# Keys and queries left unnormalised, the gate's silu moved, attention sums batched, last scaling out of place

## The chip, the cores and the metric

The kernel runs on one core of a Trainium2 chip. Its five engines work side by side, each through its own queue in order: TensorE (PE in the rows, its weight loads PEld), VectorE (DVE), ScalarE (ACT), GpSimd (POOL) and SyncE (SP, which here only issues transfers). The metric is the device time of one execution in microseconds (us).

## What is computed

One layer of a hybrid encoder for two sequences of 512 and 256 tokens, 1024 features, which share the weights. All is in float32. Cut to what matters:

```python
def _deltanet(qkv, z, ...):
    qkv = silu(centred_conv(qkv, conv_w))
    q, k = l2norm(q), l2norm(k)        # t * rsqrt(sum(t*t) + EPS), per token and head
    o = delta_direction(q, k, v, forward) + delta_direction(q, k, v, backward)
    o = o * rsqrt(mean(o * o, -1) + EPS) * norm_w
    return o * silu(z)

def _layer(x, mem, ...):
    proj = rms_norm(x, g_pre_mix) @ w_in
    att = window_attention(aq, ak, av, sink)   # window 128, softmax with one sink per head
    mix = concatenate([att, deltanet(...)], -1) @ w_out
    x = x + rms_norm(mix, g_post_mix)
    x = x + rms_norm(cross_attention(rms_norm(x, g_pre_xa), mem, ...), g_post_xa)
    h = rms_norm(x, g_pre_mlp)
    return x + rms_norm(square(relu(h @ w1)) @ w2, g_post_mlp)
```

## The kernel before, in words

The 768 tokens are six tiles of 128 (tiles 0 to 3 the first sequence, 4 and 5 the second). A large product is made of three matmuls on high and low halves of both operands (lines 187 to 189, 502 and 503, 1089 to 1091, 1165 to 1167); `split` (lines 182, 183) and the weight loader (lines 106 to 108) make these halves: ScalarE copies the high half, VectorE or GpSimd subtracts.

The body is written as generators that are merged or chained; a planner in the compiler then orders each engine's queue by program order and by when it reckons an operand to be ready. So work that stands later in the program fills gaps. The order of the stages:

1. Input norm, projections of attention's queries, keys and values, gates (0 to 97 us of the profile).
2. `proj_dn(0)`, the DeltaNet projections of heads 0 and 1, merged with `window`, the attention (97 to 230). `proj_dn` goes through keys, queries, values; for each head it projects all tokens, convolves along tokens with four VectorE multiply-adds (line 554), applies silu through tanh (557, 558), turns tiles back to token-major on TensorE (563), sums squares (571), takes the root on GpSimd (`rsqrt`, 151 and 152), normalises on VectorE (580), and turns the normalised tiles feature-major again (583, 584).
3. `deltanet(0)` chained with `proj_dn(1)` (230 to 352). `prep` makes for each pair of tiles and both directions a masked exponential E of gate sums (693, 695), multiplies the keys' Gram matrix by it (696) and the key-query product in PSUM by it (697). `inverse` inverts triangular blocks by 30 dependent VectorE steps (719, 723) and small matmuls. `step` is the scan over tiles; `dn_out` normalises its output (867 to 869) and stores it.
4. `deltanet(1)` chained with `fill` (352 to about 505): `proj_z` (the gate, with tanh, line 515 and the scaling 516), the memory's norm and keys and values. TensorE takes these while the inverse and the scan go on.
5. `tail`: output projection (`out_tile`, skewed over tiles, where line 1049 multiplies by the gate), cross-attention, and pre-norms (to 720).
6. The MLP, its second product by a Strassen scheme with seven products (720 to 1180), and `down_last` with `finish`: the last block's product is added to the accumulators (1249), squares are summed on ScalarE (1005), the sum and the root are taken on GpSimd (1007, 151, 152), the gain is multiplied in place (1260), the scaled result is added to the residual (1261) and stored.

PSUM has eight banks; in stages 2 to 4 they are tagged mm (2), tr (1), dnp (2), dns (1) and wn (2). In `window` a head's scores, their transposes and the value product share one bank, taken in turn from wn, wn and dns (line 910 the scores, 914 mask and maximum, 918 exponential, 921 transposes, 924 copy, 926 value product, 930 scaling). A ring of five tiles tagged quad holds MLP weights and at the end the gain and the residuals.

## Time and profile before

| | us |
|---|---|
| median of 3 runs (1231.92 to 1237.18) | 1232.74 |
| the profiled execution, its own time | 1231.01 |
| its span, first to last instruction | 1229.2 |
| TensorE busy | 1128.0 (92%) |
| VectorE busy | 736.4 (60%) |
| ScalarE busy | 529.3 (43%) |
| GpSimd busy | 434.7 (35%) |

The mean granted clock of TensorE is 0.967 of 2.4 GHz. Busy shares are means over stages that have different limits. In the rows, "idle before" in brackets is the time that the engine stood still before an instruction and what ended that; a wait for several things is put down to the last one. Matmuls are pipelined, so the durations of neighbours overlap. Line numbers are those of the kernel before.

### The profile page before, as it was taken

Reading aid. Unit: us, or ns where it says so; the run is one execution under the profiler, and the core shown is the slowest. Engines: PE = TensorE matmul, PEld = TensorE weight load, DVE = VectorE, ACT = ScalarE, POOL = GpSimd, SP = SyncE. Lnnn points to the kernel's source line nnn. Section 1 sums busy time; section 2 is a strip of 40 time slices with the busy share of each in tenths; the row PEclk is TensorE's granted clock in tenths of the full one; section 3 lists DMA queues with packets and bytes.
Section 4 is the critical chain, followed back from the end, with each engine's and each line's share of the span. In section 5 each row is a group of like instructions: output and inputs, shape, how many; then the busy total and the mean of one; then the engine's idle time right before and its main releaser. Section 6 shows DMA issues by size and latency. Waiting matters only on the chain.

```text
span 1229.2 us, 18098 instructions
## 1 busy us (share of the span) xinstructions
PE 1128.0 (92%) x6848; PEld 962.8 (78%) x6848; DVE 736.4 (60%) x1361; ACT 529.3 (43%) x1151; POOL 434.7 (35%) x468
## 2 busy tenths in 40 slices
PE   6998999987988799889898989999999999999994
PEld 5887788866877597578687778888888888888883
DVE  5315776799789723446534736365658565658655
ACT  5346777644565324434434534433323333233321
POOL 5353321234246423011000136343435343535461
PEclk9999999998998789899899999999999999999997
DMA  6355211311113205932722233121213122213212
GB/s 196 97 179 171 86 44 35 96 45 41 36 61 108 74 27 173 289 129 95 222 69 69 87 122 100 39 82 55 84 57 89 44 76 63 86 52 89 82 53 103
DMA packets 106931, 113.85 MB, mean 93 GB/s; under 512 B 8431, under 2 KB 80219, under 8 KB 106843
## 3 DMA queue, kind: packets, MB, share of 16 engines
q1 hardware_dynamic: 99195, 99.55, 26.8%
q10 hardware_dynamic: 7648, 13.13, 2.8%
q8 instruction: 54, 0.88, 0.3%
q14 instruction: 34, 0.28, 0.1%
HBM read 91.27 MB, written 21.39 MB: 92 GB/s over the span
## 4 chain that ended last, share of the span: by engine, by line
PE 42%; issue 4%; POOL 2%; DVE 2%; DMA 1%; ACT 1%; POOLq 0%; DVEq 0%; ACTq 0%
PE up L1165 7%; PE up L1167 7%; PE up L1166 7%; PE y L187 5%; PE y L189 5%; PE y L188 5%; POOL y L1227 1%; DMA raw<-in_xa_wo 1%; PE xa L1126 1%; PE xa L1107 1%; PE mm L1090 1%; PE mm L1091 1%; POOL rs L152 1%; PE mm L1089 1%; ACT junk L1005 0%
## 5 line engine op out<-in xcount | busy, mean ns | idle before, releaser
L108 POOL TENSOR_TENSOR wlo<-raw,whi 128x512 fp32r<-128x512 f32 (+1 forms) x61 | 88.6, 1456 | 149.2 <-ACT whi L107 100.6
L1170 POOL TENSOR_TENSOR hid<-hid 128x256 f32<-128x256 f32 (+1 forms) x64 | 60.8, 951 | 224.3 <-ACT hid L1169 224.1
L189 PE MATMUL y<-w,hl 128*128 128x512 f32 x318 | 123.9, 389 | 0.5 <-DVE hl L183 0.5
L187 PE MATMUL y<-w,hh 128*128 128x512 f32 x318 | 123.7, 389 | 0.0
L188 PE MATMUL y<-w,hh 128*128 128x512 f32 x318 | 123.7, 389 | 0.0
L1209 DVE TENSOR_TENSOR y<-y,y 128x512 f32<-128x512 f32 x72 | 48.9, 683 | 107.4 <-PE y L189 107.4
L108 DVE TENSOR_TENSOR w<-raw,w 128x1024 fp32r<-128x1024 f32 (+1 forms) x58 | 78.4, 1356 | 51.2 <-ACT w L107 51.0
L1169 ACT ACTIVATE hid<-up 128x256 f32<-128x256 f32 (+1 forms) x64 | 31.2, 488 | 179.4 <-PE up L1167 179.4
L1165 PE MATMUL up<-hx0h,w 128*128 128x512 f32 x256 | 101.2, 395 | 1.0 <-DVE hx0l L183 1.0
L1167 PE MATMUL up<-hx0h,w 128*128 128x512 f32 x256 | 100.4, 392 | 0.0
L1166 PE MATMUL up<-hx0l,w 128*128 128x512 f32 x256 | 100.1, 391 | 0.0
L971 POOL TENSOR_TENSOR quad<-quad 128x1024 f32<-128x1024 f32 x28 | 77.9, 2780 | 32.9 <-DVE w L108 14.9
L108 DVE TENSOR_TENSOR w<-quad,w 128x1024 fp32r<-128x1024 f32 x49 | 72.5, 1492 | 12.4 <-ACT w L107 12.4
L1165 PE MATMUL up<-hx4h,w 128*128 128x256 f32 x256 | 72.6, 284 | 4.5 <-ACT hid L1169 4.5
L107 ACT ACTIVATE w<-raw 128x1024 fp32r<-128x1024 f32 (+1 forms) x58 | 55.5, 964 | 43.6 <-DMA raw<-in_w_out 17.2
L1166 PE MATMUL up<-hx4l,w 128*128 128x256 f32 x256 | 72.0, 281 | 0.1
L1167 PE MATMUL up<-hx4h,w 128*128 128x256 f32 x256 | 71.8, 280 | 0.0
L189 PEld LDWEIGHTS y<-w,hl 128*128 128x128 f32 x318 | 59.7, 188 | 13.3 <-DVE hl L183 0.9
L188 PEld LDWEIGHTS y<-w,hh 128*128 128x128 f32 x318 | 59.7, 188 | 12.4
L187 PEld LDWEIGHTS y<-w,hh 128*128 128x128 f32 x318 | 59.7, 188 | 12.4
L182 ACT ACTIVATE hh<-hid 128x768 fp32r<-128x768 f32 x37 | 31.4, 848 | 81.3 <-PE y L188 64.0
L107 ACT ACTIVATE whi<-raw 128x512 fp32r<-128x512 f32 (+1 forms) x61 | 37.8, 623 | 53.1 <-DMA raw<-in_xa_wkv 10.4
(369 smaller groups left out, 3211.2 us busy)
## 6 DMA issues: line engine op xcount, KB each, us to landing
raw<-in_mlp_w SPq DMA_DIRECT2D x36, 512.0 KB, 4.4
quad<-in_mlp_w SPq DMA_DIRECT2D x28, 512.0 KB, 4.7
raw<-in_w_in SPq DMA_DIRECT2D x44, 256.0 KB, 2.9
d_x<-x ACTq DMA_DIRECT2D x12, 512.0 KB, 2.6
x<-d_x SPq DMA_DIRECT2D x12, 512.0 KB, 3.8
x<-in_x_prompt SPq DMA_DIRECT2D x8, 512.0 KB, 3.6
raw<-in_xa_wkv SPq DMA_DIRECT2D x16, 256.0 KB, 2.8
d_att<-parts SPq DMA_DIRECT2D x12, 256.0 KB, 2.0
```

The costliest lines, as they stand in the source:

```text
L107: self.nc.scalar.activation(hi[:, c], raw, AF.Copy)
L108: self.sub(out=lo[:, c], in0=raw, in1=hi[:, c].bitcast(F32), op=ALU.subtract)
L182: nc.scalar.activation(hi, src, AF.Copy)
L187: nc.tensor.matmul(ps, lh, rh, start=first, stop=False)
L188: nc.tensor.matmul(ps, lh, rl, start=False, stop=False)
L189: nc.tensor.matmul(ps, ll, rh, start=False, stop=last)
L971: nc.gpsimd.tensor_tensor(out=out, in0=x, in1=y, op=ALU.subtract)
L1165: nc.tensor.matmul(ps, wh[:, k], hh[:, k], start=k == 0, stop=False)
L1166: nc.tensor.matmul(ps, wh[:, k], hl[:, k], start=False, stop=False)
L1167: nc.tensor.matmul(ps, wl[:, k], hh[:, k], start=False, stop=k == 7)
L1170: nc.gpsimd.tensor_tensor(out=r, in0=r, in1=r, op=ALU.mult)
L1209: nc.vector.tensor_tensor(out=y, in0=y, in1=ps, op=ALU.add)
```

## The change

- `proj_dn` no longer normalises keys and queries. The product of tanh writes feature-major tiles straight into the kept buffers; the second transposes and the product of line 580 are gone. Norms of keys go as factors into the two Gram products (`na`, `a`, by scaled ScalarE copies), into the values (`rv`) and into the gate factor `kdc`; those of the queries go into the output's root in `dn_out` (`sq`).
- The product of line 697 moves from VectorE on PSUM to GpSimd on an SBUF copy.
- `proj_z` stores the raw gate; `out_tile` applies silu.
- `window`: scores are negated and masked with a minimum, so that the negation falls away; the value tiles get a column of ones, so that the value product also gives the sums; four heads share one bank (dns) for value products, and sums, sinks and scaling are done for four heads at once; scores use the two wn banks only. The load of keys and values is two loads.
- `finish` multiplies by the gain into a new tile `yg`; the gain lies in two tiles of another ring; in `rstd` the addition of two sums is a `tensor_scalar` with a pointer operand.

```diff
@@ proj_z
-        th = pool.tile([P, 770], F32, tag="tanh", bufs=1, name="th")
...
         for c, ps in zip((slice(0, 512), slice(512, 768)), out):
-            nc.scalar.activation(th[:, c], ps, AF.Tanh, scale=0.5)
-            nc.vector.scalar_tensor_tensor(out=z[:, c], in0=th[:, c], scalar=1.0, in1=ps, op0=ALU.add, op1=ALU.mult)
-        nc.gpsimd.tensor_scalar(z, z, self.nw, 0.0, ALU.mult, ALU.add)
+            nc.scalar.activation(z[:, c], ps, AF.Copy)
         nc.scalar.dma_start(self.d_z[h], z)
@@ proj_dn
-                nc.vector.scalar_tensor_tensor(out=y, in0=th, scalar=1.0, in1=y, op0=ALU.add, op1=ALU.mult)
+                dst = keep[("QhT", "KhT")[kind]][:, h] if kind < 2 else y
+                spans = [(slice(0, 512), slice(0, 512)), (slice(512, TOK), slice(514, 770))] if kind < 2 else [(slice(0, 770),) * 2]
+                for to, c in spans:
+                    nc.vector.scalar_tensor_tensor(out=dst[:, to], in0=th[:, c], scalar=1.0, in1=y[:, c], op0=ALU.add, op1=ALU.mult)
...
                     if kind == 2:
-                        nc.scalar.activation(keep["V"][:, s0:s0 + nt, h, :], ps3, AF.Copy)
+                        for t in range(nt):
+                            nc.scalar.activation(keep["V"][:, s0 + t, h, :], ps[:, t * P:(t + 1) * P], AF.Copy,
+                                                 scale=keep["rv"][:, s0 + t, h:h + 1])
                         continue
...
-                    nc.vector.tensor_tensor(out=dst, in0=ps3, in1=r.unsqueeze(2).to_broadcast([P, nt, P]), op=ALU.mult)
-                    ps = self.ps("tr")
-                    for t in range(nt):
-                        nc.tensor.transpose(ps[:, t * P:(t + 1) * P], dst[:, t], self.ident)
-                    nc.scalar.activation(dstT[:, h, s0 * P:(s0 + nt) * P], ps[:, :nt * P], AF.Copy)
+                        nc.scalar.activation(keep["Kh"][:, s0:s0 + nt, h, :], ps[:, :nt * P].rearrange("p (t f) -> p t f", f=P), AF.Copy)
+            G = nc.gpsimd
+            if kind == 1:
+                sk, a, rv = keep["sk"], keep["a"], keep["rv"]
+                G.tensor_scalar(sk, sk, EPS, 0.0, ALU.add, ALU.add)
+                G.tensor_tensor(out=a, in0=sk, in1=self.mhalf.unsqueeze(2).to_broadcast([P, NT, 2]), op=ALU.pow)
+                G.tensor_tensor(out=rv, in0=sk, in1=a, op=ALU.mult)
+                G.tensor_tensor(out=a, in0=a, in1=a, op=ALU.mult)
+                G.tensor_scalar(keep["na"], a, -1.0, 0.0, ALU.mult, ALU.add)
+                for d in range(2):
+                    kdc = self.kdc[:, :, 4 * d + 2 * half:4 * d + 2 * half + 2]
+                    G.tensor_tensor(out=kdc, in0=kdc, in1=a, op=ALU.mult)
+            elif kind == 0:
+                G.tensor_scalar(keep["sq"], keep["sq"], EPS, EPS * P * P, ALU.add, ALU.mult)
@@ prep
-        nc.scalar.activation(Gn, ps4(psG), AF.Copy, scale=-1.0)
+        for tt, t in enumerate(ts):
+            for h in range(2):
+                nc.scalar.activation(Gn[:, 2 * tt + h], ps4(psG)[:, 2 * tt + h], AF.Copy, scale=keep["na"][:, t, h:h + 1])
...
+        Pa = pool.tile([P, 4, P], F32, tag="S4", bufs=1, name="Pa")
+        for tt, t in enumerate(ts):
+            for h in range(2):
+                nc.scalar.activation(Pa[:, 2 * tt + h], ps4(psP)[:, 2 * tt + h], AF.Copy, scale=keep["a"][:, t, h:h + 1])
...
-            nc.vector.tensor_tensor(out=E[:, ds], in0=ps4(psP), in1=E[:, ds], op=ALU.mult)
+            nc.gpsimd.tensor_tensor(out=E[:, ds], in0=Pa, in1=E[:, ds], op=ALU.mult)
@@ dn_out
-        r = self.rsqrt(pool, ss, 2, 1.0 / P, EPS, "rso")
-        nc.vector.tensor_tensor(out=O, in0=O, in1=r.unsqueeze(2).to_broadcast([P, 2, P]), op=ALU.mult)
+        nc.gpsimd.tensor_tensor(out=ss, in0=ss, in1=sq[:, t], op=ALU.add)
+        nc.gpsimd.tensor_tensor(out=ss, in0=ss, in1=self.mhalf[:, 0:1].to_broadcast([P, 2]), op=ALU.pow)
+        nc.vector.tensor_tensor(out=O, in0=O, in1=ss.unsqueeze(2).to_broadcast([P, 2, P]), op=ALU.mult)
@@ window (the new loop over heads; load is cut)
+                for jj in range(2):
+                    hs = slice(4 * jj, 4 * jj + 4)
+                    nm = pool.tile([P, 4], F32, tag="nm", bufs=4, name="nm")
+                    es = pool.tile([P, 4], F32, tag="es", bufs=4, name="es")
+                    pv = self.ps("dns", "pv")[:, :260].rearrange("p (h f) -> p h f", h=4)
+                    for x in range(4):
+                        h = 4 * jj + x
+                        ps = self.ps("wn", "wS")
...
+                        nc.vector.tensor_tensor_reduce(out=sc[:, :nk * P], in0=ps[:, :nk * P], in1=mk, scale=-0.125,
+                                                       scalar=self.nsink[:, h:h + 1], op0=ALU.add, op1=ALU.min,
+                                                       accum_out=nm[:, x:x + 1])
+                        nc.scalar.activation(sc[:, :nk * P], sc[:, :nk * P], AF.Exp, bias=nm[:, x:x + 1], scale=-1.0)
...
+                        for b in range(nk):
+                            nc.tensor.matmul(pv[:, x], pT[:, b], vs[:, k0 + b, jj], start=b == 0, stop=b == nk - 1)
+                        yield
+                    nc.gpsimd.tensor_tensor(out=es, in0=nm, in1=self.sink[:, hs], op=ALU.add)
+                    nc.scalar.activation(es, es, AF.Exp)
+                    nc.vector.tensor_tensor(out=es, in0=pv[:, :, 64], in1=es, op=ALU.add)
+                    nc.vector.reciprocal(es, es)
+                    nc.vector.tensor_tensor(out=o[:, hs], in0=pv[:, :, 0:64], in1=es.unsqueeze(2).to_broadcast([P, 4, 64]), op=ALU.mult)
@@ rstd
-            nc.gpsimd.tensor_tensor(out=ss[:, 0:1], in0=ss[:, 0:1], in1=ss[:, 1:2], op=ALU.add)
+            nc.gpsimd.tensor_scalar(ss[:, 0:1], ss[:, 0:1], ss[:, 1:2], 0.0, ALU.add, ALU.add)
@@ out_tile
+        th = pool.tile([P, 4, P], F32, tag="b2", bufs=3, name="zth")
+        nc.scalar.activation(th, zt, AF.Tanh, scale=0.5)
+        nc.vector.scalar_tensor_tensor(out=zt, in0=th, scalar=1.0, in1=zt, op0=ALU.add, op1=ALU.mult)
...
-        nc.vector.tensor_tensor(out=zt, in0=zt, in1=pz.rearrange("p (k c) -> p k c", k=4), op=ALU.mult)
+        nc.vector.scalar_tensor_tensor(out=zt, in0=pz.rearrange("p (k c) -> p k c", k=4), scalar=self.nw, in1=zt,
+                                       op0=ALU.mult, op1=ALU.mult)
@@ down_last
-        gain = self.w2pool.tile([P, D], F32, tag="quad", bufs=5, name="gain")
-        nc.sync.dma_start(gain, self.a["norm_post_mlp"][0].partition_broadcast(P))
+        gain = [pool.tile([P, 512], F32, tag="S", bufs=2, name="gain", padded_shape=[P, 768]) for _ in range(2)]
+        for j in range(2):
+            nc.sync.dma_start(gain[j], self.a["norm_post_mlp"][0][512 * j:512 * j + 512].partition_broadcast(P))
@@ finish
+        yg = self.w2pool.tile([P, D], F32, tag="quad", bufs=5, name="yg")
         r = self.rstd(pool, [ya, yb])
         for j, y in enumerate((ya, yb)):
             c = slice(512 * j, 512 * j + 512)
-            nc.vector.tensor_tensor(out=y, in0=y, in1=gain[:, c], op=ALU.mult)
-            nc.vector.scalar_tensor_tensor(out=x[:, c], in0=y, scalar=r, in1=x[:, c], op0=ALU.mult, op1=ALU.add)
+            nc.vector.tensor_tensor(out=yg[:, c], in0=y, in1=gain[j], op=ALU.mult)
+        for j in range(2):
+            c = slice(512 * j, 512 * j + 512)
+            nc.vector.scalar_tensor_tensor(out=x[:, c], in0=yg[:, c], scalar=r, in1=x[:, c], op0=ALU.mult, op1=ALU.add)
             nc.sync.dma_start(self.row(t)[1][:, c], x[:, c])
```

## Rows read from the trace of the kernel before

**Rows 1.** Head of the page: span; engines' busy us, share, instructions.

```profile
span 1229.2 us, 18098 instructions
...
PE 1128.0 (92%) x6848; PEld 962.8 (78%) x6848; DVE 736.4 (60%) x1361; ACT 529.3 (43%) x1151; POOL 434.7 (35%) x468
```

**Rows 2.** Busy us by stretch: stretch, length, PE, PEld, DVE, ACT, POOL, clock, DMA.

```profile
97.00:230.00 133.00, 126.40 (x879) 110.14 (x878) 89.40 (x326) 99.05 (x310) 32.40 (x37) 1.00 0.26 78
230.00:302.00 72.00, 60.83 (x420) 51.79 (x420) 68.32 (x172) 36.96 (x81) 25.47 (x23) 0.93 0.24 60
...
352.00:420.00 68.00, 52.33 (x347) 43.89 (x345) 65.89 (x158) 36.63 (x82) 40.95 (x36) 0.85 0.26 86
...
480.00:583.00 103.00, 91.70 (x425) 73.15 (x424) 46.05 (x66) 38.30 (x73) 10.20 (x25) 0.97 0.57 186
...
1175.00:1230.00 55.00, 35.81 (x154) 28.31 (x153) 31.91 (x42) 11.27 (x27) 22.55 (x27) 0.87 0.22 77
```

**Rows 3.** Waits of TensorE, 230 to 302 and 352 to 420: us, times, longest.

```profile
PE tr L583 <- DVE room L580: 7.8, 3, 5.6
...
PE wn L187 <- DVE z L515: 5.6, 1, 5.6
PE mm L502 <- DVE z L515: 3.6, 1, 3.6
PE tp L381 <- DVE z L515: 2.7, 1, 2.7
```

**Rows 4.** Timelines of VectorE and TensorE, 470 to 510: start, length, instruction [idle before].

```profile
476.01 0.43 DVE L869 TENSOR_TENSOR O<-O,rs 128x256 f32<-128x256 f32 x1 [0.87 <-POOL rs L152]
...
497.73 0.40 PE L187 MATMUL wn<-hm,whi 128*128 128x512 f32 x1
...
505.46 0.79 PE L187 MATMUL mm<-w,hx4h 128*128 128x512 f32 x1 [0.57 <-ACT hx4h L182]
```

**Rows 5.** Timeline of VectorE in the final scaling, tile 3 of 6, and the end.

```profile
1199.40 0.68 DVE L1249 TENSOR_TENSOR yc<-yc,y 128x512 f32<-128x512 f32 x1
1200.93 0.69 DVE L1260 TENSOR_TENSOR yc<-yc,gain 128x512 f32<-128x512 f32 x1 [0.85 <-ACT junk L1005]
1201.54 0.68 DVE L1249 TENSOR_TENSOR y<-y,y 128x512 f32<-128x512 f32 x1
...
1204.75 0.75 DVE L1261 SCALAR_TENSOR_TENSOR x<-yc,rs,x 128x512 f32<-128x512 f32 x1 [0.99 <-POOL rs L152]
...
1224.85 1.41 DVE L1261 SCALAR_TENSOR_TENSOR x<-y,rs,x 128x512 f32<-128x512 f32 x2 [1.00 <-POOL rs L152]
```

**Rows 6.** Timeline of GpSimd for the same tile.

```profile
1203.11 0.70 POOL L1007 TENSOR_TENSOR ss<-ss 128x1 f32<-128x1 f32 x1 [5.08 <-ACT junk L1005]
1203.89 0.19 POOL L151 TENSOR_SCALAR rs<-ss 128x1 f32<-128x1 f32 x1
1204.17 0.55 POOL L152 TENSOR_TENSOR rs<-rs,mhalf 128x1 f32<-128x1 f32 x1
```

**Rows 7.** Line 515's own view: ns min/median/max, first and last start.

```profile
L515 DVE SCALAR_TENSOR_TENSOR z<-th,mm x4: 406/542/678, 370.5 to 386.8; 128x512 f32<-128x512 f32 x2, 128x256 f32<-128x256 f32 x2
```

**Rows 8.** VectorE's groups, 230 to 480: count, busy us, mean ns, idle.

```profile
L697 DVE TENSOR_TENSOR E<-dnp,E 128x512 f32<-128x512 f32 x12 | 7.9, 678 | 0.0
```

**Rows 9.** Timeline of TensorE: first transposes of two and of four tiles.

```profile
227.39 0.44 PE L563 MATMUL tr<-ident,y 128*128 128x128 f32 x2 [0.16 <-DVE y L558]
...
228.30 0.66 PE L563 MATMUL tr<-ident,y 128*128 128x128 f32 x4
```

**Rows 10.** Timelines of VectorE and GpSimd, first tile of the final scaling.

```profile
1183.11 1.69 DVE L1260 TENSOR_TENSOR yc<-yc,gain 128x512 f32<-128x512 f32 x1 [0.79 <-ACT junk L1005]
...
1182.96 3.00 POOL L1227 TENSOR_TENSOR y<-y,y 128x512 f32<-128x512 f32 x2
```

**Rows 11.** Timelines of TensorE and ScalarE: scores and copy of the last head.

```profile
218.94 0.48 PE L910 MATMUL wS<-kT,qT 128*128 128x256 f32 x2
...
222.81 0.39 ACT L924 ACTIVATE pT<-wS 128x256 f32<-128x256 f32 x1 [0.70 <-PE wS L921]
```

79 lines of the change are left out of this document (31 added, 48 removed).

## The prediction, made before the change was run

> **What bounds the kernel now.** I read four views in this order. First the head of the page: TensorE is busy for 1128.0 of 1229.2 us [rows 1], so at most about 101 us of the span is TensorE standing still, and a change that only lightens other engines can win no more than a part of that, plus what TensorE work it takes away. Second the table by stages, to see where these 101 us lie [rows 2]: the reader should subtract the TensorE column from the length of each stretch. 97 to 230 us (windowed attention beside the first half's projections) loses 6.6 us; 230 to 302 (preparation and triangular inverse of the first half) loses 11.2; 352 to 420 (the same for the second half) loses 15.7; 1175 to 1230 (last block and final scaling) loses 19.2. In the second and the third of these VectorE is busy for 68.3 of 72 and 65.9 of 68 us: it is the bound there and TensorE waits behind it. Third the waits of TensorE inside these two stretches [rows 3]: 7.8 us in three waits of the second transposes (line 583) for VectorE's normalised tile (line 580), and 5.6, 3.6 and 2.7 us, 11.9 together, for line 515, the gate's product that frees a PSUM bank. Fourth the end of the middle part in order of time [rows 4]: VectorE's last product of the scan starts at 476.01 us, while TensorE still multiplies memory keys and values until 497.73 + 0.40, and the output projection starts at 505.46. So at the end of the middle TensorE is 21.7 us behind the scan. There the time that TensorE lost earlier counts, and not VectorE's chain.
>
> The final scaling is another case. VectorE's rows for one tile [rows 5] are: add the first half, wait 0.85 for ScalarE's square, multiply by the gain, add the second half, wait 0.85 again, multiply, wait 0.99 for GpSimd's root, scale. The waits of 0.85 are there because line 1260 writes the tile that ScalarE is squaring. Line 1261 of this tile starts at 1204.75 and that of the last tile, three tiles on, at 1224.85: 6.70 us a tile. TensorE needs less: the row of its stretch shows 35.8 us busy of 55 [rows 2].
>
> **The change part by part.** *Final scaling.* The product with the gain goes to a tile of its own, so both waits for ScalarE's square go; the number of instructions stays. A tile then takes, from start to start of the VectorE rows [rows 5], add 0.61, product 0.61, add 0.61 (the gap from 1199.40 to 1200.93 less its wait leaves 0.68 for the full row, 0.61 when the next follows at once: 1200.93 to 1201.54), then the root's latency, then two scalings of 0.75 less overlap, 1.34. The root's latency from the end of the second add, 1201.54 + 0.68 = 1202.22, to the end of GpSimd's power, 1204.17 + 0.55 = 1204.72, is 2.50 us [rows 5, 6]. In it the sum of the two squares took 0.70; it becomes an instruction of the kind of line 151, which took 0.19, so 2.0. The second product, 0.61, fits inside. Sum 1.83 + 0.07 + 2.0 + 1.34 = 5.2, and with the semaphore gaps of these rows 5.3. Five tiles follow the first one, whose root waits for GpSimd's additions as before: 5 x (6.70 - 5.3) = **7.0 us**. If the planner also puts the next tile's adds ahead of the scaling, a tile falls to TensorE's own pace and the gain reaches 10; if it keeps them apart, 5. The new tile takes a second slot of the five-slot ring at each step; the slot it takes was last read by line 1261 two tiles earlier, and the load of the residual now waits for a store three tiles, some 16 us, back. The gain's two loads instead of one stand on SP's queue well before.
>
> *The gate.* Eight products of line 515 (0.54 each in the middle, four of them in [rows 7], the other four alike), 4.3 us, leave VectorE's chain in 352 to 420, and four GpSimd scalings with them. The bank is now freed by a ScalarE copy of the same length as the tanh it replaces, and ScalarE is busy for 36.6 of these 68 us [rows 2]. So the 11.9 us of waits go. In the output projection six tanh and six products of 512 columns come in, about 0.7 us each by the nearest product (line 697, [rows 8]): 8 us on two engines that are busy 46.1 and 38.3 of 103 us beside a TensorE with 91.7 [rows 2]. That work covers them; they run ahead of the tile's transposes, and without the cover the first tile would pay 0.7 + 0.7 = 1.4 us once.
>
> *Unnormalised keys and queries.* 48 second transposes leave TensorE, 24 in each half. Two transposes take 0.44 and four 0.66 [rows 9], so each further one 0.11: 2.6 us a half. The product (line 580) leaves VectorE's queue, and with it the wait for GpSimd's root. Of the 7.8 us of [rows 3] I count 3, from 0 to 7.8: VectorE stays the bound there, so TensorE is likely to stand one step later, at the first transposes, behind the convolution's taps. ScalarE loses the copy of line 584, gains one for the keys, splits the values' copy by tile and takes four scaled copies for one, twice per tile pair; it is busy for 37.0 of 72 us there [rows 2]. Seven tiny GpSimd operations per half are off every path, as the values and the gates are used much later.
>
> *Products moved to GpSimd.* Twelve products of line 697, 7.9 us together [rows 8], leave VectorE. They read PSUM and one SBUF tile. The new ones read two SBUF tiles on GpSimd, and there a price appears: a product of line 1260 took 1.69 us while GpSimd ran line 1227, against 0.69 without [rows 5, 10]. So each move costs VectorE up to 1.0 us where it issues products of two SBUF tiles, and gives 0.66: between -7.9 and +4.1 us on VectorE's chain; I take +4.1, as preparation is full of such products. With the gate's 4.3 that makes the second half's chain even to a little shorter. The Trainium skill, in "GPSIMD Engine Reference" (section Specifications), says that GpSimd shares its SBUF interfaces with VectorE and contends with VectorE instructions that read two SBUF inputs. By that rule this move works against the change, and the trace agrees (1.69 against 0.69 us, [rows 5, 10]). Were every moved product to hold VectorE for its whole length, an estimate by the shortest of the GpSimd rows, 3.00 for two, the move would cost 12 x (1.5 - 0.66) = 10 us.
>
> *Middle together.* TensorE's end moves by 11.9 + 3 + 2.6 = **17.5 us**. The scan's chain leaves room for it: it ends 21.7 us earlier now, and by its own sum it does not get longer by more than 4. Ends: 4 (the chain takes over) and 28 (all 7.8 us, and the lost clock, below).
>
> *Attention.* Per head three small VectorE operations and one small exponential go, and the sums come from a column of ones in the value product; the scores now turn in two banks instead of three, and four heads' value products share the third. In 97 to 230 TensorE is the bound, 126.4 of 133 [rows 2]. 24 transposes, 2.6 us, go for certain; of the 6.6 us of idle time I count 1.4. **4 us**, from -7 to +8 (the two banks, below). Six more loads stand on SP's queue, each a part of what was one load before.
>
> The profiled execution took 1231.01 us, 1.8 more than its span, and 1.7 less than the median of 1232.74. 1231.0 - 7.0 - 17.5 - 4 = 1202.5; with the 1.7 a median of **1204**.
>
> **The rivals.** *The chain takes over the middle.* VectorE is the bound in both preparations, and if GpSimd's products stretch them, TensorE's waits come back at the first transposes and the end hangs on the scan. Then the middle gives 4 and attention 2.6: 1232.7 - 7 - 4 - 2.6 = 1219. For it: 68.3 of 72 us; against it: the 21.7 us by which TensorE ends later. *More than that.* The granted clock is 0.85 of 2.4 GHz in 352 to 420 [rows 2], so for 2 x 0.15 x 68 = 20 us TensorE was at 1.2 GHz, in the stretch in which it waits most. Without the waits it may stay at 2.4: the middle gives 28, attention 7, the end 9.5: 1188. *The waits only change names.* The final product waits for the root instead, the transposes for the taps, and the new slots bring back what the out-of-place tile takes away: 1231. *Two banks.* The last head holds its score bank from 218.94 to 222.81 + 0.39, 4.26 us [rows 11]. Two banks and 48 heads make 24 x 4.26 = 102 us, inside the stretch of 133. From a mean hold of 5.5 us this becomes the bound; every 0.1 us more costs 2.4. At 7.0 us the stretch grows by 24 x 1.5 = 36 us, which eats the 28.5 of the rest: 1240. Against it: the hold gets shorter by the dropped operations, and two heads in flight queue less than three.
>
> **How the numbers follow.** The forecast, 1204 (1195 to 1213), has 0.48; the chain, 1219 (1213 to 1226), 0.22; more, 1188 (1178 to 1195), 0.17; names only, 1231, 0.08; two banks, 1240, 0.05. A range from 1188 to 1226 leaves out half of the third case and the last two, about 2 in 10. A measurement of this kernel tells 0.5%, 6.2 us, from no change: faster than 1226.6 is 0.48 + 0.22 + 0.17 = 0.87, the same 0.08, slower than 1238.9 0.05.
>
> **What would show it.** Final scaling: no wait of VectorE for ScalarE's square, and scalings of successive tiles 5.3 us apart. Gate: no TensorE wait on line 515's successor in the second inverse, and TensorE's last memory product some 20 us earlier, close to the scan's end. GpSimd's products: VectorE's mask operations of 0.3 us turned into ones over 1 us. Attention: few waits of a score product for its bank, and a stretch that ends by about 226. Wrong would be a scan that ends later than 476, waits of TensorE on VectorE's taps as long as those that went, or a weight load of the output projection that stays at 482 us.

## The result and the profile after

The change makes the kernel faster: a median of 1219.47 us (1217.75 to 1221.22, 4 runs) against 1234.96 us (1231.92 to 1238.18, 4 runs). The ratio is 0.9874 with a 95% interval from 0.984 to 0.9909, so 15.5 us or 1.3%. The prediction had said 1204, which is 28.7 us below the median that it started from; about half of that came. Executions more than 1.5% above the fastest one of the same kernel are left out of the ratios here and below, but not out of the medians. The two profiled executions are 1231.01 and 1220.31 us, 10.7 apart; the difference between 15.5 and 10.7 is mostly scatter of the kernel before (below).

The head of the page of the changed kernel, which answers [rows 1]: span, then busy us, share and instructions of each engine.

```profile
span 1218.5 us, 17803 instructions
...
PE 1117.1 (92%) x6800; PEld 955.7 (78%) x6800; DVE 706.6 (58%) x1183; ACT 530.5 (44%) x1123; POOL 438.7 (36%) x475
```

TensorE is busy for 10.9 us less and the span is 10.7 us shorter: it stands still for as long as before, 101.4 us. The prediction had counted on shorter waits. The table by stages, with the columns of [rows 2], shows where it stands still now.

```profile
97.00:230.00 133.00, 130.52 (x892) 114.60 (x892) 69.96 (x173) 91.42 (x242) 36.82 (x42) 0.99 0.29 85
230.00:302.00 72.00, 55.53 (x380) 47.35 (x378) 70.05 (x166) 42.05 (x107) 32.28 (x27) 0.88 0.18 48
352.00:420.00 68.00, 46.91 (x474) 39.14 (x474) 57.69 (x140) 39.35 (x96) 36.79 (x37) 0.85 0.23 73
480.00:583.00 103.00, 91.25 (x423) 72.44 (x422) 51.50 (x73) 42.94 (x82) 11.69 (x27) 0.97 0.54 174
1175.00:1230.00 55.00, 30.76 (x136) 25.10 (x134) 26.33 (x37) 8.69 (x24) 16.30 (x25) 0.88 0.28 96
```

In the attention (97 to 230) TensorE has 2.5 us idle instead of 6.6. In the first preparation and inverse (230 to 302) the idle time is 16.5 instead of 11.2, and VectorE is busy for 70.05 us, more than the 68.32 before, although six of the twelve moved products lie here. In the second (352 to 420) it is 21.1 instead of 15.7. The waits of TensorE in these two stretches, which answer [rows 3]:

```profile
PE tr L567 <- DVE room L562: 12.1, 2, 6.3
...
PE dnp L764 <- DVE C L741: 10.3, 1, 10.3
PE mm L504 <- ACT z L515: 6.3, 1, 6.3
```

At the first transposes the kernel before had waited for less (waits of TensorE, 230 to 302):

```profile
PE tr L563 <- DVE y L558: 3.0, 1, 3.0
```

The 7.8 us of the second transposes are gone, and 12.1 us at the first transposes, 3.0 before, stand in their place. They are for the product of tanh behind the convolution's taps (line 562). In VectorE's queue the planner has put it among the steps of the first inverse (lines 734 and 738), so it comes late:

```profile
287.50 0.18 DVE L738 TENSOR_TENSOR A<-A,t 128x32 f32<-128x32 f32 x1
287.61 0.69 DVE L562 SCALAR_TENSOR_TENSOR room<-tanh,y 128x512 f32<-128x512 f32 x1
```

Of the 11.9 us for the gate's product 6.3 are left, now for ScalarE's plain copy, and 10.3 us for the second inverse (line 741 is the transpose at its end, on VectorE) are new.

The end of the middle, TensorE's timeline. The scan's last product on VectorE starts at 468.66, 7.4 us earlier than in [rows 4], but the memory's keys and values end at 499.3, where they ended before to within a microsecond, and the output projection starts 2.0 us earlier:

```profile
498.95 0.39 PE L189 MATMUL wn<-hm,wlo 128*128 128x512 f32 x1
...
503.43 0.50 PE L187 MATMUL mm<-w,hx4h 128*128 128x512 f32 x1 [0.25 <-ACT hx4h L182]
```

The final scaling is as forecast. VectorE's scalings of two successive tiles and of the last one, against [rows 5]; GpSimd's sum of squares against [rows 6]:

```profile
1192.07 1.42 DVE L1294 SCALAR_TENSOR_TENSOR x<-yg,rs,x 128x512 f32<-128x512 f32 x2 [1.45 <-POOL rs L152]
...
1197.58 1.42 DVE L1294 SCALAR_TENSOR_TENSOR x<-yg,rs,x 128x512 f32<-128x512 f32 x2 [1.45 <-POOL rs L152]
...
1214.10 1.41 DVE L1294 SCALAR_TENSOR_TENSOR x<-yg,rs,x 128x512 f32<-128x512 f32 x2 [1.44 <-POOL rs L152]
```

```profile
1196.33 0.30 POOL L1032 TENSOR_SCALAR ss<-ss 128x1 f32<-128x1 f32 x1 [4.29 <-ACT junk L1030]
```

No wait for ScalarE's square is left, the period is 5.51 us (it was 6.70, 5.3 was forecast), and the sum takes 0.30 instead of 0.70.

### The profile page after: what moved, and what is told of

Read it like the earlier page. It is cut to its first block, busy times and chain, and to the rows that moved or that the text cites. A ratio compares the mean times of both kernels' runs of the same rounds, so it can differ in the third digit from the quotient of the medians.

```text
span 1218.5 us, 17803 instructions
## 1 busy us (share of the span) xinstructions
PE 1117.1 (92%) x6800; PEld 955.7 (78%) x6800; DVE 706.6 (58%) x1183; ACT 530.5 (44%) x1123; POOL 438.7 (36%) x475
## 4 chain that ended last, share of the span: by engine, by line
PE 47%; DMA 4%; issue 3%; DVE 3%; POOL 3%; ACT 2%; ACTq 0%; POOLq 0%; DVEq 0%; SPq 0%
PE up L1194 7%; PE up L1195 7%; PE up L1196 7%; PE y L189 5%; PE y L187 5%; PE y L188 5%; DMA raw<-in_w_out 2%; PE mm L189 2%; PE mm L187 2%; PE mm L188 2%; POOL y L1256 1%; DVE w L108 1%; DMA raw<-in_xa_wo 1%; ACT w L107 1%; PE xa L1155 1%
## 5 line engine op out<-in xcount | busy, mean ns | idle before, releaser
L108 POOL TENSOR_TENSOR wlo<-raw,whi 128x512 fp32r<-128x512 f32 (+1 forms) x61 | 83.6, 1374 | 137.2 <-ACT whi L107 98.6
L996 POOL TENSOR_TENSOR quad<-quad 128x1024 f32<-128x1024 f32 x28 | 77.4, 2764 | 33.2 <-DVE w L108 20.6
L108 DVE TENSOR_TENSOR w<-quad,w 128x1024 fp32r<-128x1024 f32 x49 | 72.6, 1492 | 12.5 <-ACT w L107 12.5
L107 ACT ACTIVATE w<-raw 128x1024 fp32r<-128x1024 f32 (+1 forms) x58 | 55.5, 963 | 38.5 <-DMA raw<-in_w_out 14.1
L107 ACT ACTIVATE whi<-raw 128x512 fp32r<-128x512 f32 (+1 forms) x61 | 37.9, 625 | 50.3 <-DMA raw<-in_xa_wkv 12.3
```

Of the source, the lines that this page charges most:

```text
L107: self.nc.scalar.activation(hi[:, c], raw, AF.Copy)
L108: self.sub(out=lo[:, c], in0=raw, in1=hi[:, c].bitcast(F32), op=ALU.subtract)
L996: nc.gpsimd.tensor_tensor(out=out, in0=x, in1=y, op=ALU.subtract)
```

## Experiments

**How they are compared.** Each kernel ran beside the kernel before on the same chip, on three chips in all. Executions of one program differ by up to 22 us here: the kernel before took from 1221.0 to 1242.9 us. Its time follows the mean granted clock of TensorE, which is listed for each execution (1221.0 us at 0.977, 1242.9 at 0.955). One straight line for 124 executions of the twelve kernels below and of the kernel before beside them (those that the ratios use), with one offset per kernel, gives 0.81 us for each 0.001 of the clock, and leaves 1.9 us of scatter. So two numbers stand for each kernel: the measured ratio, and its time at the clock 0.965, worked out with that line (standard error 0.3 for the kernel before, 0.7 to 1.1 for the others). The changed kernel's four executions (mean 1219.5 at 0.9645) give 1219.1.

Three things limit these numbers. One execution lies 10.4 us off the line, the profiled one of finish_only (1227.31 us at 0.951). Its records list a clock of 0.95 over long stretches in which TensorE does the same work in the same time: from 97 to 230 it is busy for 126.20 us, against 126.40 at 1.00 in [rows 2].

```profile
97.00:230.00 133.00, 126.20 (x874) 109.98 (x873) 89.44 (x326) 98.93 (x310) 32.37 (x37) 0.95 0.25 76
```

Without this execution the line has 0.88 us for each 0.001, finish_only's gain falls from 6.1 to 4.1 us, and the other gains move by less than 0.9. Next, the clock is in part an outcome of an edit, and a low clock costs little while TensorE waits anyway (rows further down). So a gain at equal clock says where time may have come from, and the measured ratio says what came. Last, finish_only has the same order of instructions as the kernel before on TensorE, VectorE and ScalarE up to 1150 us, and its output projection still starts 2.7 us later (508.12 against 505.46). So a start that moves by less than 3 us between two profiled executions tells nothing.

| kernel | median us | ratio to before, 95% | clock, 305 to 325 | clock, 420 to 440 | us at clock 0.965 | against before |
|---|---|---|---|---|---|---|
| before | 1230 to 1236 | 1 | 1.00 | 0.60 | 1232.5 | |
| the change | 1219.47 | 0.9874, 0.984 to 0.9909 | 0.61 | 1.00 | 1219.1 | -13.4 |
| finish_only | 1229.19 | 0.9951, 0.9901 to 1.0001 | 0.87 | 0.64 | 1226.4 | -6.1 |
| gate_only | 1222.09 | 0.9937, 0.9902 to 0.9972 | 1.00 | 1.00 | 1228.6 | -3.9 |
| window_only | 1236.76 | 1.002, 0.9985 to 1.0055 | 0.59 | 0.57 | 1229.4 | -3.1 |
| norms_only | 1224.14 | 0.9943, 0.9896 to 0.9989 | 1.00 | 0.52 | 1223.4 | -9.1 |
| e_on_vector | 1212.9 | 0.9849, 0.9784 to 0.9915 | 0.51 | 0.99 | 1213.1 | -19.4 |
| memory_ahead | 1222.52 | 0.9933, 0.9894 to 0.9972 | 0.90 | 0.50 | 1218.5 | -14.0 |
| weight_slots | 1212.65 | 0.9845, 0.9767 to 0.9924 | 0.62 | 1.00 | 1214.3 | -18.2 |
| window_as_before | 1216.15 | 0.9887, 0.9841 to 0.9932 | 0.50 | 0.98 | 1217.8 | -14.7 |
| norms_in_exponent | 1209.99 | 0.9813, 0.9777 to 0.9849 | 0.51 | 0.96 | 1214.4 | -18.1 |
| exponent_and_slots | 1207.86 | 0.981, 0.9765 to 0.9855 | 1.00 | 1.00 | 1211.4 | -21.1 |
| exponent_slots_old_window | 1194.99 | 0.9697, 0.9656 to 0.9739 | 1.00 | 1.00 | 1204.2 | -28.3 |
| best_more_ahead | 1198.37 | 0.9699, 0.964 to 0.9758 | 1.00 | 0.51 | 1202.4 | -30.1 |

The two columns of the clock are of the profiled execution, in the 20 us that follow the small matmuls of the first and of the second inverse. TensorE is busy there for 18.1 to 20.0 of 20 us in every kernel, so a clock of 0.50 loses it up to 10 us of work.

**The parts alone.** Four kernels, each the kernel before with one part of the change.

finish_only takes over the three edits of `down_last`, `finish` and `rstd`, as in the diff.

> The kernel before with only the edit of the final scaling (product with the gain out of place, gain in two tiles, sum of squares by tensor_scalar). Theory (the final scaling carries most of the gain, the rest of the change little): 7 to 9 us faster than the kernel before, scalings of successive tiles 5.5 us apart, everything up to 1175 us as before. Rival (the gain is spread, the middle carries it): 2 to 4 us faster at most, and the rest of the change is worth over 10.

From the start of the first scaling to that of the last it is 28.21 us as in the changed kernel, 34.15 before: 5.94 us. The whole time agrees, but tells less: 6.0 us by the ratio (0 to 12), 6.1 or 4.1 at equal clock. So the final scaling is worth some 6 us, between theory and rival, and the rest of the change 7 to 9 at equal clock.

gate_only takes over the edits of `proj_z` and `out_tile`.

> The kernel before with only the gate's edit (raw gate stored, silu in the output projection). The prediction's own count: TensorE's 11.9 us of waits for line 515's product go, the output projection starts some 10 us before 505.46, whole time -9 to -12. Theory D (in the middle a wait that goes comes back at the next place, since VectorE, ScalarE's queue and the granted clock set the pace of the stretch): the three waits for the product are replaced by waits for the scan's small matmuls and for copies on ScalarE of about the same sum; the output projection starts within 3 us of 505.46, whole time 0 to -3.

The three waits for the gate's product are gone, and one for the inverse has their size (line 723 is the transpose at the inverse's end there), from the waits of TensorE, 352 to 420:

```profile
PE dnp L746 <- DVE C L723: 12.5, 1, 12.5
```

The output projection starts at 501.24, 4.2 us earlier, and at equal clock 3.9 us are won, by the ratio 7.8 (3.4 to 12.1). The whole time alone would not rule out the count of 11.9; the wait of 12.5 us in the place of the three does. Theory D holds in its main point, that the wait comes back; it named other places (the scan's matmuls and copies), and the numbers lie a little outside its own.

window_only takes over the new `window`.

> The kernel before with only the attention's edit. Both theories: scores end some 5 us earlier (219.1 before, 214.1 in the changed kernel). The prediction's count: the stretch gives 4 to 5 us to the end, the output projection starts at 500 to 501.5. Theory D: the preparation of the first half starts 3 us earlier at most, since it waits for the broadcast loads of the gate sums, the output projection starts within 2 us of 505.46; whole time 0 to -2.

The scores end at 215.46, 3.7 us earlier, the first half's preparation starts 2.2 us earlier, and yet the output projection starts at 513.53, 8.1 us later: outside both expectations. The planner now puts a gate's product, which had started at 385.97, behind most of the second inverse in VectorE's queue, so the memory's transposes wait for it (waits of TensorE, then in a second fence VectorE's timeline):

```profile
PE tp L383 <- DVE z L517: 13.8, 1, 13.8
```

```profile
407.98 0.68 DVE L517 SCALAR_TENSOR_TENSOR z<-th,mm 128x512 f32<-128x512 f32 x1
```

But that is 13.8 in the place of 11.9. The larger part of the 8.1 us goes with the clock, which falls after both inverses (rows below). At equal clock the attention wins 3.1 us, about what its own stretch shows; by the ratio nothing is won (from 1.8 us faster to 6.8 slower).

norms_only takes over the unnormalised keys and queries, with E's product on GpSimd.

> The kernel before with only the unnormalised keys and queries and the products of E on GpSimd. The prediction's count: 2.6 us of transposes a half and 3 us of waits go, whole time -3 to -8. Theory D with GpSimd's contention: from the first mask operation to the first T copy the first half takes 69 to 70 us (66.4 before, 69.5 in the changed kernel), mask operations with a GpSimd product beside them mean 1.0 us, the output projection starts within 3 us of 505.46; whole time +2 to -3.

The mask operations mean 0.555 us and the preparation and inverse of the first half get longer, 72.6 us from 224.05 to 296.67 (66.4 before), more than expected. But it starts 6.4 us earlier, since the second products and transposes are gone from the attention's stretch as well, and the output projection starts at 499.25, 6.2 us earlier, where theory D expected at most 3. At equal clock it wins 9.1 us, by the ratio 7.0 (1.4 to 12.8): theory D was too low here. This part alone also takes most of the gate's waits. Of the 11.9 us for line 515, 4.3 are left (waits of TensorE, 352 to 420), but the wait for the low half of a weight on GpSimd is 5.5, which was 2.0:

```profile
PE mm L189 <- POOL wlo L108: 5.5, 1, 5.5
PE wn L503 <- DVE z L515: 3.1, 1, 3.1
...
PE wn L187 <- DVE z L515: 1.2, 1, 1.2
```

**GpSimd's products.** e_on_vector puts one line of the changed kernel back:

```diff
-            nc.gpsimd.tensor_tensor(out=E[:, ds], in0=Pa, in1=E[:, ds], op=ALU.mult)
+            nc.vector.tensor_tensor(out=E[:, ds], in0=Pa, in1=E[:, ds], op=ALU.mult)
```

> The changed kernel with the twelve products of E back on VectorE (still from the copy Pa in SBUF). TensorE's queue then has 47 memory matmuls ahead of the second inverse's matmuls (line 764) instead of 6. Theory A (the supply of memory weights sets the end of the middle): the mask operations fall back from a mean of 1.0 us under a GpSimd product to 0.34, the chain may be 3 to 5 us shorter, but the output projection still starts within 2 us of 503.4; whole time 0 to -2 us against the changed kernel. Theory B (TensorE's wait of 10.3 us ahead of line 764 sets it): that wait goes, the output projection starts 6 to 10 us earlier, whole time -6 to -10. Theory C (contention alone costs the chain): inverse ends 3 to 5 us earlier in both halves, whole time -3 to -5.

The mask operations of the first half in VectorE's groups (count, busy us, mean ns, idle before and what ended it), in the changed kernel with GpSimd's products below, and then in this one:

```profile
L708 DVE SCALAR_TENSOR_TENSOR E<-E,cole,emask 128x128 f32<-128x128 f32 x24 | 12.8, 600 | 5.4 <-DMA E<-d_gc 5.4
...
L712 POOL TENSOR_TENSOR E<-Pa,E 128x512 f32<-128x512 f32 x6 | 9.9, 1657 | 7.8 <-DVE L L711 4.1 <-DMA E<-d_gc 1.9 <-ACT E L710 1.8
```

```profile
L708 DVE SCALAR_TENSOR_TENSOR E<-E,cole,emask 128x128 f32<-128x128 f32 x24 | 7.6, 386 | 5.3 <-DMA E<-d_gc 5.3
```

From the first mask operation to the last it is 12.3 us instead of 15.0, though VectorE does the products as well. So in the first half the move costs VectorE 12.8 - 7.6 = 5.2 us on these 24 operations and saves it six products of 0.68, 4.1 us. In the second half it costs nothing there: the 24 mask operations take 0.389 us in the mean in the changed kernel and 0.407 in this one. Over the whole execution VectorE is busy for 706.6 us in the changed kernel and as long in this one, with twelve products more on it:

```profile
PE 1121.4 (93%) x6800; PEld 959.8 (79%) x6800; DVE 706.1 (58%) x1195; ACT 529.9 (44%) x1123; POOL 427.4 (35%) x463
```

The whole is 6.0 us faster at equal clock, and the output projection starts at 498.00, 5.4 us earlier. That is a little over what theory C expected, but not by its mechanism: the inverse's small matmuls start 1.8 us earlier in the first half (293.93 against 295.71) and 3.2 us later in the second (414.25 against 411.08), where theory C had 3 to 5 us earlier in both. With the product on VectorE the planner also places 47 instead of 6 memory matmuls ahead of the second inverse, and the wait there falls from 10.3 to 8.8 us. Theory A, which expected at most 2 us, falls; theory B's wait did not go. What brought the 6.0 us is open.

**TensorE's order and the memory's weights.** memory_ahead changes the program order of the changed kernel:

```diff
-        run(self.deltanet(dn, 1, keep1), self.fill(cv, m0, k0))
+        delta, fill = self.deltanet(dn, 1, keep1), self.fill(cv, m0, k0)
+        for _ in range(7):
+            next(delta)
+        for _ in range(45):
+            next(fill)
+        run(delta, fill)
```

> The changed kernel with 45 steps of the filling work put ahead of the second inverse in program order, so that 39 memory matmuls instead of 6 stand ahead of line 764 in TensorE's queue; GpSimd's products stay. Theory A (weight supply): TensorE's wait ahead of line 764 falls from 10.3 to under 4 us, but the output projection starts within 2 us of 503.4 and the whole time moves by 0 to -2 us against the changed kernel. Theory B (TensorE's order): -5 to -9 us. Theory C (contention): no change of the time, since the products stay on GpSimd.

The wait ahead of the inverse goes, and a new one stands behind its first group of matmuls, for the copy that the second group reads (waits of TensorE, 395 to 425):

```profile
PE dnp L776 <- ACT Z L772: 7.2, 1, 7.2
PE dnp L769 <- DVE C L746: 1.9, 1, 1.9
```

The output projection starts 3.8 us later, the clock in 420 to 440 is 0.50 instead of 1.00, and at equal clock the kernel is 0.6 us faster, which is inside the error; the median is 3.1 us slower. Theory B, that the wait of 10.3 us sets the end, falls; theory A had the time about right, but not the later start.

weight_slots gives the memory's weights two more landing tiles:

```diff
+                    if self.spare and self.n % 2:
+                        raw = self.spare.tile([P, D], F32, tag="x", bufs=2, name="raw")[:, :(c.stop - k) * n].rearrange("p (k n) -> p k n", n=n)
+                    else:
+                        raw = pool.tile([P, c.stop - k, n], F32, tag="raw", bufs=bufs, name="raw")
...
+        self.W.spare = m0
         yield from self.proj_z(pool, 3)
```

> The changed kernel with two more landing slots for the memory's weights (the tiles of the memory's norm, free by then, take every other load), everything else as it is, TensorE's order ahead of line 764 too (6 memory matmuls). Theory A (weight supply): memory kv ends 4 to 8 us earlier than 498.9 and the first loads of the output projection's weights earlier than 482.98; whole time -3 to -8 us against the changed kernel. Theory B (TensorE's order) and C (contention): 0 to -2 us.

SyncE issues the first load of the output projection's weights, in the changed kernel and then in this one, at

```profile
482.98 0.34 SPq L106 DMA_DIRECT2D raw<-in_w_out  x1
```

```profile
470.67 0.34 SPq L110 DMA_DIRECT2D raw<-in_w_out  x1
```

Memory keys and values end at 496.0, 3.3 us earlier, the output projection starts only 0.8 earlier, and the MLP's first product starts 6.5 earlier (646.84 against 653.35). So most of the gain, 4.8 us at equal clock, comes behind the start of the output projection, whose own weights are there sooner: the supply of weights is a part of what holds the kernel, as theory A says, but not the whole.

**Norms in the exponent.** norms_in_exponent leaves out the scaled copies: a factor on a row of both Gram products is a summand in the exponent that both are multiplied by.

```diff
-                G.tensor_scalar(keep["na"], a, -1.0, 0.0, ALU.mult, ALU.add)
+                nc.scalar.activation(keep["na"], sk, AF.Ln)
...
+                    cole = self.cole[:, :, 4 * d + 2 * half:4 * d + 2 * half + 2]
+                    G.tensor_tensor(out=cole, in0=cole, in1=keep["na"], op=ALU.add)
...
-        for tt, t in enumerate(ts):
-            for h in range(2):
-                nc.scalar.activation(Gn[:, 2 * tt + h], ps4(psG)[:, 2 * tt + h], AF.Copy, scale=keep["na"][:, t, h:h + 1])
+        nc.scalar.activation(Gn, ps4(psG), AF.Copy, scale=-1.0)
...
-            nc.gpsimd.tensor_tensor(out=E[:, ds], in0=Pa, in1=E[:, ds], op=ALU.mult)
+            nc.vector.tensor_tensor(out=E[:, ds], in0=ps4(psP), in1=E[:, ds], op=ALU.mult)
```

> The changed kernel with the keys' norms as a logarithm in the exponent of the mask (added to the column that line 711 subtracts), so that the 24 scaled copies of each half's Gram products on ScalarE are 3 plain ones, no copy Pa is made, and the product of E is on VectorE from PSUM as in the kernel before. Theory C and D (contention and ScalarE's queue lengthen the preparation): mask operations back to 0.34 us, first mask operation to first T copy 64 to 67 us in the first half, whole time -5 to -10 against the changed kernel. Rival (the preparation is not what sets the end): the stretch gets shorter but the output projection starts within 2 us of 503.4.

The mask operations of the first half mean 0.389 us, near the 0.34 that were expected. The preparation and inverse of the first half take 69.0 us (227.24 to 296.28), not 64 to 67. The output projection starts at 493.06, 10.4 us earlier than in the changed kernel, and at equal clock it is 4.7 us faster; the rival falls. But the kernel is no faster than e_on_vector at equal clock (1214.4 and 1213.1), so no run shows the copies on ScalarE as a cost of their own.

**Putting parts together.** window_as_before is the changed kernel with the old `window`. exponent_and_slots is norms_in_exponent with the slots of weight_slots. exponent_slots_old_window has the old `window` besides.

> The changed kernel with the attention as in the kernel before; everything else of the change stays. TensorE's queue then has 44 memory matmuls ahead of the second inverse's matmuls instead of 6. Theory E (the parts add up: the attention's edit alone cost 5.7 us of span, because the planner's order of the second half gets worse, though its own stretch gets 4 us shorter): scores end some 4 us later than 214.1, the output projection starts 3 to 6 us earlier than 503.4, whole time -4 to -8 against the changed kernel. Rival (the loss of the attention's edit alone came from the gate's product on VectorE, which the full change doesn't have; in the full change the 4 us arrive at the end): whole time +2 to +5.

> The kernel with the norms in the exponent and two more landing slots for the memory's weights. If the supply of weights still paces the end of the middle there: memory kv ends 2 to 4 us earlier than 487.8, whole time -2 to -4 against the kernel with the norms in the exponent alone. If the chain of the second half does (its scan ends at 472.8, TensorE waits 13.1 us ahead of line 760): 0 to -1.

> As the kernel with the norms in the exponent and two more landing slots, with the attention as before. TensorE's order ahead of the second inverse is nearly the same with either attention here (65 and 68 memory matmuls). Theory E in its narrow form (the attention's edit costs only through that order): the 4 us of its own stretch arrive, so this kernel is 2 to 5 us slower than the one with the new attention. In its wide form (the edit costs wherever it stands): 3 to 7 us faster.

window_as_before is 1.3 us faster than the changed kernel at equal clock: neither -4 to -8 nor +2 to +5. In the full change the attention's edit is worth about nothing. exponent_and_slots wins 3.0 us at equal clock over norms_in_exponent, as expected where weights pace the end; the memory's keys and values end 7.5 us earlier there (481.1), more than the 2 to 4 expected. exponent_slots_old_window is 7.2 us faster than with the new attention at equal clock (12.9 by the medians): the wide form of theory E. It is the fastest kernel, 3.0% faster than the kernel before; what in the new attention costs 7.2 us there was not found.

best_more_ahead asks whether the wait ahead of the second inverse can be filled at all. It is exponent_slots_old_window with the edit of memory_ahead, 72 steps instead of 45.

> The fastest kernel so far (norms in the exponent, two more landing slots, attention as before) with the filling work put ahead of the second inverse in program order, so that 120 memory matmuls instead of 68 stand ahead of the inverse's first matmuls in TensorE's queue. There TensorE waits 17.6 us for the inverse. Theory F (what TensorE loses in the second half is the time from the end of the work placed ahead of the inverse to the inverse's end, under whatever name it is listed): 52 more matmuls of 0.234 us are 12 us of work, the wait falls to 2 to 6 us, the output projection starts 6 to 12 us earlier than 483.8, whole time -6 to -12 against that kernel. Rival (the wait moves on to the copies between the inverse's matmuls and to the memory's weights, as when 39 matmuls were put ahead in the changed kernel): the wait goes and the output projection starts within 3 us of 483.8.

The waits of TensorE, 352 to 484, in exponent_slots_old_window and in best_more_ahead:

```profile
PE dnp L763 <- DVE C L740: 13.7, 1, 13.7
```

```profile
PE mm L191 <- ACT whi L111: 6.0, 1, 6.0
PE dnp L775 <- ACT Z L771: 5.2, 1, 5.2
```

The second half's wait is 13.7 us; the 17.6 of the expectation are those of both inverses. 13.7 us of one wait are 11.2 us of two others, and the output projection starts at 486.36, 2.6 us later: the rival. Theory F falls. At equal clock the kernel is 1.8 us faster, with an error of 1.5; its median is 3.4 us slower, and the ratios to the kernel before beside each are the same (0.9699 and 0.9697). So the edit is worth nothing that these runs can tell.

**The clock.** The rows of 305 to 325 and of 420 to 440 (stretch, length, TensorE, its loads, VectorE, ScalarE, GpSimd, granted clock, DMA). The kernel before:

```profile
305.00:325.00 20.00, 19.64 (x246) 17.02 (x233) 14.27 (x22) 10.91 (x32) 4.33 (x7) 1.00 0.17 41
420.00:440.00 20.00, 18.52 (x260) 15.24 (x260) 5.23 (x12) 5.20 (x11) 1.27 (x1) 0.60 0.09 28
```

The changed kernel:

```profile
305.00:325.00 20.00, 20.00 (x236) 17.52 (x227) 10.61 (x17) 8.13 (x19) 2.00 (x3) 0.61 0.07 19
420.00:440.00 20.00, 20.00 (x192) 17.24 (x190) 6.26 (x16) 7.30 (x15) 3.73 (x4) 1.00 0.14 40
```

gate_only:

```profile
305.00:325.00 20.00, 19.91 (x328) 17.61 (x326) 14.24 (x20) 11.01 (x32) 5.77 (x7) 1.00 0.15 38
420.00:440.00 20.00, 19.93 (x283) 17.41 (x274) 6.63 (x16) 7.57 (x16) 3.32 (x4) 1.00 0.09 29
```

window_only:

```profile
305.00:325.00 20.00, 20.00 (x144) 17.60 (x143) 8.36 (x13) 9.33 (x29) 2.19 (x5) 0.59 0.03 7
420.00:440.00 20.00, 20.00 (x253) 16.44 (x249) 5.76 (x12) 6.22 (x15) 4.59 (x4) 0.57 0.14 48
```

best_more_ahead:

```profile
420.00:440.00 20.00, 18.11 (x249) 14.67 (x250) 5.29 (x10) 5.38 (x11) 0.00 (x0) 0.51 0.15 42
```

The reader is to see the third number from the end of each row, the granted clock. The kernel before has TensorE at 1.2 GHz for most of the stretch after the second inverse, the changed kernel after the first, window_only after both, gate_only after neither. By length times what the clock lacks, that is 20 x 0.40 = 8.0 us of TensorE's work in the kernel before, 20 x 0.39 = 7.8 in the changed one, 16.8 in window_only and none in gate_only. In these two executions the change won 8 us in one place and lost 8 in the other.

Each kernel was profiled once, and the clock is not a matter of the order of instructions alone. finish_only, whose order is that of the kernel before up to here, has the same fall behind the second inverse, and besides a stretch at half clock behind the first, where the kernel before has none:

```profile
307.00:310.00 3.00, 3.00 (x20) 2.53 (x17) 2.91 (x5) 0.98 (x2) 0.00 (x0) 0.50 0.34 87
...
420.00:440.00 20.00, 18.29 (x284) 14.36 (x273) 6.49 (x12) 7.36 (x13) 2.87 (x4) 0.64 0.13 41
```

What TensorE did before a fall: in the second half it had stood still once more between the inverse's groups of small matmuls. From 5 to 10 us after the first of these matmuls it is idle for 0.8 to 5.0 us in the six kernels whose clock then falls (1.3 in the kernel before, 5.0 in memory_ahead), and for 0.07 to 0.55 us in the eight where it is at 2.4 GHz from 420 to 440. In these eight it had fallen before that. They have one long wait ahead of the inverse, 7.9 to 14.1 us, and none behind it, and the half clock lies in that wait and in the first small matmuls after it, where TensorE has little to lose. In the changed kernel:

```profile
405.00:416.00 11.00, 4.92 (x102) 3.85 (x103) 10.83 (x40) 4.64 (x6) 2.33 (x4) 0.53 0.01 2
```

So the two groups differ in where the half clock lies, in a wait or in work. window_only has a wait of 13.8 us too, but ahead of the memory's transposes, and there the clock is at half in both places. In the first half the idle time behind the first small matmuls doesn't separate the kernels: with 1.7 us idle at that place exponent_and_slots stayed at 1.00, norms_in_exponent with 2.0 fell to 0.51. No kernel was made to test a cause, so what decides it is open.

## Why the prediction was half right

**The time.** 1204 was forecast with 1195 to 1213 around it; 1219.47 lies above that, and in the range from 1188 to 1226 only because this takes in the first rival. It is the time that this rival gave, but only half by its mechanism. TensorE's waits did come back at the first transposes, as it said. But the scan's chain was to set the end of the middle; in the trace the scan ends at 468.7 and TensorE's memory product at 499, 30 us behind, where it was 21.7 behind before. That 1219 was hit so closely is luck.

**The terms, each alone.** The forecast's transposes are put with the edit that removes them: 2.6 us in each half belong to keys and queries, though the prediction adds those of the first half under attention. The last column is the ratio of the experiments, in us, with the half width of its 95% interval.

| term | forecast us | alone, at equal clock | alone, by the ratio |
|---|---|---|---|
| final scaling | -7.0 | -6.1 | -6.0 ± 6.2 |
| gate | -11.9 | -3.9 | -7.8 ± 4.3 |
| unnormalised keys and queries | -8.2, with +4.1 on VectorE's chain taken as hidden | -9.1 | -7.0 ± 5.7 |
| attention | -1.4 | -3.1 | +2.5 ± 4.3 |
| sum | -28.5 | -22.2 | -18.3, some 10 either way |
| the change as a whole | | -13.4 | -15.5 ± 4.3 |

*Final scaling* was right in mechanism and size: the period of 5.51 us against 5.3 differs by the sum of the two squares (0.30 instead of 0.19) and the gaps between semaphores. *Attention* was right for its own stretch: two banks did not become the bound, TensorE's waits from 97 to 230 name no score bank, and the scores end 5.0 us earlier in the full change. That this gain reaches the end is not shown: alone it is 3.1 us at equal clock and nothing by the ratio, and in the full change it is nothing either way (window_as_before). *Keys and queries* came out near the count. The wait of the second transposes went, the one at the first transposes grew as the prediction feared, and the attention's stretch got shorter by more than the 2.6 us of its transposes: the first mask operation starts 6.4 us earlier in norms_only.

*The gate is the step that failed.* "So the 11.9 us of waits go" took the name in the list of waits for the cause. TensorE stood there for a PSUM bank, but behind these waits little other work was left in its queue ahead of the second inverse, and the inverse, some 30 dependent steps on VectorE, wasn't over; line 515 stood among these steps. VectorE's timeline in the kernel before, where line 723 is a step of the inverse:

```profile
410.07 0.18 DVE L723 TENSOR_TENSOR A<-A,t 128x32 f32<-128x32 f32 x1
410.18 0.68 DVE L515 SCALAR_TENSOR_TENSOR z<-th,wn 128x512 f32<-128x512 f32 x1
```

Without it the wait is for the inverse, 12.5 us in gate_only. In the full change 6.3 us for ScalarE's copy and 10.3 for the inverse stand there. The prediction looked for what is late next at the end of the middle only, and not at this place. That the scan ended 21.7 us before TensorE did not help either: the second half's waits lie before the scan starts.

*GpSimd's products* were priced too high: +4.1 us on VectorE's chain were forecast. The mask operations alone give 5.2 - 4.1 = 1.1 in the first half and no price in the second, and VectorE's busy time over the whole execution, which has the price on its other operations too, is the same with the move and without it (706.6 and 706.1 us). So in sum the move gave VectorE nothing and cost it nothing. A second flaw is that the price was put on a chain with 21.7 us of room. In 230 to 302 VectorE has none: TensorE waits 12.1 us there for the product of tanh. The Trainium skill says in "GPSIMD Engine Reference" (section Specifications) that GpSimd shares its SBUF interfaces with VectorE and contends with its instructions that read two SBUF inputs; the trace agrees in the first half, with 0.600 against 0.386 us for the same mask operation, and shows no difference in the second. How much of the 6.0 us of e_on_vector is this and how much the planner's other order was not told apart.

*The sum.* At equal clock the parts alone give 22.2 us and together 13.4 (20.6 and 13.5 without finish_only's outlying execution). By the ratios it is 18.3 and 15.5, with an error of some 10, so the measured times alone do not show that the parts fail to add up. Two overlaps show in the runs: norms_only alone leaves 4.3 of the gate's 11.9 us of waits, so these two parts take the same waits; and the attention's 3.1 us are worth nothing in the full change (window_as_before). The 6.0 us of e_on_vector are no such piece, since norms_only has GpSimd's products too. The order of each queue is the planner's, and each part changes it for the others: 39 memory matmuls stand ahead of the second inverse in the kernel before, 5 in window_only, 52 in norms_only, 6 in the changed kernel.

*The clock* was in the prediction only as the rival "more", which had TensorE stay at 2.4 GHz without the waits. The profiled executions show rather the reverse in the second half: kernels that keep one long wait ahead of the inverse have the full clock in the work after it, and those that fill it (memory_ahead, best_more_ahead) have half of it for 20 us. The change as a whole kept its mean clock, 0.965 against 0.967 in the profiled executions.

*ScalarE's tanh in the output projection* was counted as covered by other work, with 1.4 us at most if not. It stands in ScalarE's queue between the memory's weights and waits for its own load, and TensorE waits behind it for the copy kvo. ScalarE's timeline, then TensorE's:

```profile
480.98 0.63 ACT L107 ACTIVATE whi<-raw 128x512 fp32r<-128x512 f32 x1 [4.02 <-DMA raw<-in_xa_wkv]
484.33 0.63 ACT L1069 ACTIVATE zth<-zt 128x512 f32<-128x512 f32 x1 [2.71 <-DMA zt<-d_z]
...
485.38 0.58 ACT L401 ACTIVATE kvo<-wn 128x512 f32<-128x512 f32 x1
```

```profile
486.01 1.11 PE L407 MATMUL tr<-ident,kvo 128*128 128x128 f32 x4 [4.16 <-ACT kvo L401]
```

At the same place the kernel before waited for 2.05 us. A moved step brings its place in the queue with it, not only its duration.

*What would show it.* The final scaling's signs came as said. "TensorE's last memory product some 20 us earlier" did not. Six of the 24 mask operations of the first half turned into ones over 1 us, where two were before. Of the signs that the prediction had named as wrong, two came: the first weight load of the output projection stayed at 482.98, and the wait behind the taps (12.1 us) is longer than the one that went (7.8).

## What to carry to other kernels

A wait in a list of waits carries the name of the last thing that was late. Before counting it as won, look for what the same engine would wait for next at that place, and how much work stands ahead of it in the queue.

On a TensorE-bound kernel look at the granted clock beside the time: one 20 us stretch at half clock is 8 to 10 us, as much as most single edits. Give the measured ratio with it, since the clock is in part what the edit did, and in part it differs between executions of one order. A factor that scales rows of a masked exponential can go into its exponent: that made 24 copies of a half on ScalarE three plain ones, though no run shows time won by it alone. An operation moved to GpSimd must be charged to VectorE's two-input operations that run beside it.

## What the runs showed of the hardware

The time of one program follows the mean granted clock, 0.81 us per 0.001 of it over all kernels, from 1221.0 us at 0.977 to 1242.9 at 0.955 for the kernel before, with the same program. One execution breaks this by 10.4 us: records of 0.95 over long stretches did not make TensorE slower there. Why the clock differs between executions was not found.

The mask operation on VectorE, two SBUF tiles of 128x128, took 0.35 us in the median and up to 1.39 beside GpSimd's operations on 128x512. The six long ones of the first half each end 0.15 us after a GpSimd operation ends; for four that is a product of E, for two a subtraction for weights (line 108). Three of them, with GpSimd's operations beside them:

```profile
238.19 4.00 DVE L708 SCALAR_TENSOR_TENSOR E<-E,cole,emask 128x128 f32<-128x128 f32 x3
```

```profile
237.75 2.98 POOL L712 TENSOR_TENSOR E<-Pa,E 128x512 f32<-128x512 f32 x2 [3.46 <-DVE L L711]
240.69 1.35 POOL L108 TENSOR_TENSOR wlo<-raw,whi 128x512 fp32r<-128x512 f32 x1
```

GpSimd's product took 1.66 us in the mean in the first half; the same product on VectorE, read from PSUM, 0.68.
